# Differential attention's scores as three float32r products of split q and k

## The chip, the cores and the metric

One core of a Trainium2 chip runs the whole program. The metric is device time in microseconds (us) of one execution, lower is better; the profile is one execution, recorded instruction by instruction. TensorE (PE) multiplies matrices, VectorE (DVE) and ScalarE (ACT) work on rows, GpSimd (POOL) does very little here, and SyncE (SP) issues most of the DMAs that bring the weights from memory.

## What is computed

Two layers of a decoder trunk on 256 tokens of width 2048. In each layer one projection `w_in` feeds three kinds of head (differential attention, a gated linear recurrence "lru", chunked linear attention "gla"), one projection `w_out` joins them, and a SwiGLU feed-forward part follows. What the change touches is the scores of the differential attention, two maps `m` for each of 8 heads:

```python
q_d = rope(q_d.reshape(B, S, DIFF_HEADS, 2, DIFF_HD), pos)      # DIFF_HD = 64
k_d = rope(k_d.reshape(B, S, DIFF_HEADS, 2, DIFF_HD), pos)
...
s = jnp.einsum('bhmqd,bhmkd->bhmqk', q_blk * d ** -0.5, kh)     # q blocks of 128 rows
s = jnp.where(kpos[None, :] <= qpos[:, None], s, -jnp.inf)
p = jax.nn.softmax(s, axis=-1)
a = p[:, :, 0] - lam * p[:, :, 1]
o = rms_norm(jnp.einsum('bhqk,bhkv->bhqv', a, vh), subln_w) * (1.0 - lam_init)
```

## The kernel before

**Products.** Every large product is written as three float32r products: a float32 operand x is split into hi = float32r(x), made by ACT, and lo = x - hi, made by DVE, and hi·hi + hi·lo + lo·hi is summed in PSUM. `block` (lines 417 to 419) does this for one 512-wide (twice 264-wide) block of weights, 16 chunks of 128 rows, for the two token tiles t = 0, 1 in turn: six products a chunk. The tiles `hilo` hold the split weights, `split` makes them some 7 chunks ahead, and each costs ACT one cast and DVE one subtraction. A layer's input side is 12 such blocks ("in"); four blocks "op" of the output projection follow, chunks 0 to 7 of which read the attention's rows of `yh`, `yl`, chunks 8 to 11 the lru's and chunks 12 to 15 the gla's.

**Mixers.** Attention, lru and gla are generators (`head`, `norm`, `lru_x`, `lru_g`, `gla_gates`, `gla_out`, ...) whose steps are put between the products of the blocks. `rotated` transposes the rotated rows of q and of k (`tpq`), and ACT copies them to `s` tiles in float32. `head` (four heads in each of two groups g, two query tiles qt) multiplies q and k in float32 into `sps` (line 873), two maps on rows 0 to 63 and 64 to 127 of the array, adds the mask, takes exponentials (`e`), transposes them (`tpa`) and multiplies with v (`po`). At the layer's end `lru_g` transposes gate rows (`tp_lg`), multiplies (`lru`) and splits into `yh`, `yl` chunks 8 to 11; `gla_out` makes `pog` (two tiles), the squares of it on ACT (`junk`), the inverse root on DVE (`rs_v`, `rs_q`, `rr`), scaled rows (`ong`), the transpose (`tpog`) and the split into chunks 12 to 15.

**What sets the order.** A planner (`Lane`) runs while the program is written down. It keeps a clock `lane.clk`, which every PE step advances by an estimate of its cost, and an estimate of when DVE and ACT are free; after each unit of a block it lets the generators whose time has come issue their next step. The hardware's queues then run each engine's instructions in exactly that written order. So an estimate in the planner moves instructions, though nothing on the chip reads it. `lane.require` writes down a step at once when a block needs its result.

The score step and its estimate are:

```python
for m in range(2):
    r0 = slice(64 * m, 64 * m + 64)
    nc.tensor.matmul(sps[:, m, :nk], qT[r0, h, qt * P:(qt + 1) * P],
                     kT[r0, h, :nk], start=True, stop=True)
lane.clk += 0.45 if qt == 0 else 0.88
```

Of the kernel before, what the change touches and what calls it, by code (L numbers as in the profile page):

```python
# [10 lines left out]
F32 = mybir.dt.float32  # L11
F32R = mybir.dt.float32r
# [7 lines left out]
P = 128  # L20
S = 256
# [171 lines left out]
def tile_hybrid_trunk(ctx, tc, x, xT, w_in, w_out, w_gu, w_down, post_norms, lams,  # L193
                      vecs, wbd, w_gup, ropes, out):
    nc = tc.nc
    PS = bass.MemoryType.PSUM
    lane = Lane()
    done = lane.done
    dve, act = Engine(lane, nc.vector, 0.1, 1.04e-3), Engine(lane, nc.scalar, 0.1, 0.83e-3)
# [66 lines left out]
    for l in range(DEPTH):  # L266
# [5 lines left out]
        for kind, f, b in ffn_order():  # L272
# [4 lines left out]
            recipes, i = [], 0  # L277
# [300 lines left out]
    def parts(name):  # L578
        return pm.tile([P, DC, S], F32R, tag="big", name=name, bufs=5)

    def s4(name):
        return pm.tile([P, 4, S], F32, tag="s4", name="s4", bufs=NS4)

    def wide(name, tag="rp"):
        return pm.tile([P, 512], F32, tag=tag, name=name, bufs={"rp": 3, "e": 2, "on": 1}[tag])
# [154 lines left out]
    for l in range(DEPTH):  # L740
        lam_init = 0.8 - 0.6 * math.exp(-0.3 * l)
        sc, s2 = new_scale()
        yh, yl = None, None


        nlam = pt.tile([P, 1], F32, tag="nlam", name="nlam", bufs=2)
# [81 lines left out]
        def small(name, *needs):  # L828
            if name not in tiles:
                lane.require(*needs)  # L830
                tiles[name] = s4(name)
            return tiles[name]

        def rows(name, *needs):

            return small(name, *needs).rearrange("p a b -> p (a b)").rearrange("p (t n) -> p t n", t=NT)

        def rotated(made, scale, name):

            for t in range(NT):  # L840
                yield dve.through(0.25, "tr") if t == 0 else act.through(0.0, "tr")
                tp = turned(made[t], "tr", name="tpq")
                act.mul(small(name)[:, :, t * P:(t + 1) * P], tp, scale)
                act.drops("tr")
            done[name] = True

        def scaled(func, dst=None):
# [7 lines left out]
        def attention(g, qt):  # L855


            nk = (qt + 1) * P
            rsum = pt.tile([P, 4, 2], F32, tag="rsum", name="rsum")
            ssq = pt.tile([P, 4], F32, tag="ssq", name="ssq")  # L860
            po = []

            def head(h):
                prev = (l, g, qt, h - 1) if h else (l, g, 0, 3) if qt else (l, g - 1, 1, 3)
                yield 0.3, None, lane.has((l, "q", g), (l, "k", g), (l, "v", g), (l, "small"), (prev, "s"))
                yield 0.0, "sc", lambda: lane.use["e"] < 2
                done[(l, g, qt, h), "s"] = True
                lane.use["e"] += 1
                qT, kT, v = tiles[l, "q", g], tiles[l, "k", g], rows((l, "v", g))
                sps = pp.tile([P, 2, 512], F32, tag="sc", name="sps", bufs=1)  # L870
                for m in range(2):
                    r0 = slice(64 * m, 64 * m + 64)
                    nc.tensor.matmul(sps[:, m, :nk], qT[r0, h, qt * P:(qt + 1) * P],
                                     kT[r0, h, :nk], start=True, stop=True)
                lane.clk += 0.45 if qt == 0 else 0.88
                yield after(0.3)
                dve.tensor_tensor(out=sps[:, :, qt * P:nk], in0=sps[:, :, qt * P:nk],
                                  in1=cmask[:, None, :].to_broadcast([P, 2, P]), op=ALU.add)
                nm = pt.tile([P, 2], F32, tag="nm", name="nm")
                dve.tensor_reduce(out=nm, in_=sps[:, :, :nk], axis=AX.X, op=ALU.max, negate=True)  # L880
                yield dve.through()
                e = wide("e", "e").rearrange("p (m k) -> p m k", m=2)
                esum = pt.tile([P, 2], F32, tag="esum", name="esum")
                for m in range(2):
                    act.activation(e[:, m, :nk], sps[:, m, :nk], AF.Exp, bias=nm[:, m:m + 1],
                                         accum_out=esum[:, m:m + 1])
                act.drops("sc")
                yield act.through()
                dve.reciprocal(rsum[:, h, :], esum)
                yield NOW  # L890
                ncf = pt.tile([P, 1], F32, tag="ncf", name="ncf")
                dve.scalar_tensor_tensor(out=ncf, in0=esum[:, 0:1], scalar=nlam,
                                               in1=rsum[:, h, 1:2], op0=ALU.mult, op1=ALU.mult)
                yield NOW
                dve.scalar_tensor_tensor(out=e[:, 0, :nk], in0=e[:, 1, :nk], scalar=ncf,
                                               in1=e[:, 0, :nk], op0=ALU.mult, op1=ALU.add)
                yield dve.through(W_SM, "tr", lambda: lane.use["aT"] < 2)
                lane.use["aT"] += 1
                tp = pp.tile([P, 2, P], F32, tag="tr", name="tpa", bufs=1)
                for kt in range(qt + 1):  # L900
                    nc.tensor.transpose(tp[:, kt, :], e[:, 0, kt * P:(kt + 1) * P], ident)
                lane.use["e"] -= 1
                lane.clk += 0.11 * (qt + 1)
                aT = pt.tile([P, 2, P], F32, tag="aT", name="aT", bufs=2)
                act.copy(aT[:, :qt + 1, :], tp[:, :qt + 1, :])
                act.drops("tr")
                yield act.through(W_AT, ("o" if h == 0 else None), lane.has((prev, "av")))
                if h == 0:
                    po.append(pp.tile([P, 4, P], F32, tag="o", name="po", bufs=1))
                for kt in range(qt + 1):  # L910
                    nc.tensor.matmul(po[0][:, h, :], aT[:, kt, :], v[:, kt, h * P:(h + 1) * P],
                                     start=(kt == 0), stop=(kt == qt))
                lane.use["aT"] -= 1
                done[(l, g, qt, h), "av"] = True
                lane.clk += 0.22 * (qt + 1)
                yield after(0.3)
                junk = pt.tile([P, 512], F32, tag="junk", name="junk", bufs=1)[:, :P]
                act.activation(junk, po[0][:, h, :], AF.Square, accum_out=ssq[:, h:h + 1])
                yield act.through()
                done[(l, g, qt, h), "end"] = True  # L920

            def norm():
                yield 0.0, None, lane.has(*(((l, g, qt, h), "end") for h in range(4)))
                r0sq = pt.tile([P, 4], F32, tag="r0sq", name="r0sq", bufs=2)
                dve.tensor_tensor(out=r0sq, in0=rsum[:, :, 0], in1=rsum[:, :, 0], op=ALU.mult)
                rr = pt.tile([P, 4], F32, tag="rr", name="rr", bufs=2)
                yield NOW
                yield from rsqrt(rr, ssq, 4, 1.0 / P, pre=r0sq)
                dve.tensor_tensor(out=rr, in0=rr, in1=rsum[:, :, 0], op=ALU.mult)
                yield NOW  # L930
                on = wide("on", "on")
                dve.tensor_tensor(out=on.rearrange("p (h d) -> p h d", h=4), in0=po[0],
                                        in1=rr[:, :, None].to_broadcast([P, 4, P]), op=ALU.mult)
                dve.drops("o")
                yield dve.through(0.25, "tr")
                tp = turned(on, "tr", name="tpo")
                sl = slice(qt * P, (qt + 1) * P)
                split_scaled(yh[:, 4 * g:4 * g + 4, sl], yl[:, 4 * g:4 * g + 4, sl], tp, subw)
                dve.drops("tr")
                done[l, "y", g, qt] = True  # L940

            done[(l, -1, 1, 3), "s"] = done[(l, -1, 1, 3), "av"] = True
            for h in range(4):
                lane.add(10 + 2 * g + qt + h / 8, head(h))
            lane.add(9, norm())
# [63 lines left out]

        def lru_g(made, tiles):  # L1010
            for t in range(NT):
                yield act.through(0.25, "tr", lane.has((l, "hs")))
                hs = tiles["hs"]
                tp = turned(made[t], "tr", name="tp_lg")
                sl = slice(t * P, (t + 1) * P)
                dve.tensor_tensor(out=hs[:, :, sl], in0=hs[:, :, sl], in1=tp, op=ALU.mult)
                dve.drops("tr")
                yield dve.through()
                split_scaled(yh[:, 8:12, sl], yl[:, 8:12, sl], hs[:, :, sl], None)
                done[l, "lru", t] = True  # L1020
# [175 lines left out]
        for g in range(2):  # L1196
# [22 lines left out]
                    lane.add(6, small_parameters())  # L1219
                in_block(each(0, rotate, rotated, 1.0, (l, "k", g)), B_K[g][0])  # L1220
            in_block(each(0, scaled(AF.Copy, lambda t: rows((l, "v", g))[:, t, :]), ready, (l, "v", g)), B_V[g][0])
            if g == 0:
                yh, yl = parts("yh"), parts("yl")
            for qt in range(NT):
                attention(g, qt)
        in_block(each(4, scaled(AF.Copy), lru_x, tiles), B_LX[0])
# [274 lines left out]
```

## Time and profile before

| | us |
|---|---|
| median of three runs | 2192.33 (2191.77 to 2193.1) |
| the profiled execution's own time | 2193.04 |
| its span, first to last instruction | 2191.3 |
| PE busy | 2162.1 |
| DVE busy | 1814.0 |
| ACT busy | 1372.6 |

PE is the engine of the chain that ended last: the page puts 88% of that chain on PE and 8% on DVE. The granted clock is 0.999 of full speed throughout. "Busy" of PE counts products whose ends are modelled and which overlap, so the starts of successive products tell more than their lengths: a row that starts later than the usual step after the one above it marks a place where PE did not stream.

### The profile page before, as it was taken

How to read it: one execution, taken by the hardware profiler on the slowest of the kernel's cores; microseconds unless marked ns; L12 is line 12 of the kernel's file. 1: busy time of each engine (PE TensorE's matmuls, PEld its weight loads, DVE VectorE, ACT ScalarE, POOL GpSimd, SP SyncE). 2: the span in 40 equal slices, each digit the busy share in tenths (PEclk: the TensorE clock that was granted, in tenths of full speed). 3: DMA queues.
4: the chain of work that ended last, by engine and by line, in shares of the span. 5: the costliest groups of instructions: out<-in, count | busy, mean ns of one | idle time of the engine just before them, and what ended most of it. 6: DMA issues, size and time to landing. Idle time of an engine off the chain costs nothing.

```text
span 2191.3 us, 30890 instructions
## 1 busy us (share of the span) xinstructions
PE 2162.1 (99%) x10052; PEld 1769.5 (81%) x10052; DVE 1814.0 (83%) x3373; ACT 1372.6 (63%) x2715; POOL 96.1 (4%) x128
## 2 busy tenths in 40 slices
PE   8999999999999999999999999999999999999998
PEld 6778878887888888888877788788878888888886
DVE  6776965898999999999786668668989999999985
ACT  6556755676666666666565567557666666666663
POOL 0000000000000000000000000000000000000000
PEclk9999999999999999999999999999999999999999
DMA  8653646677877777777645536565777877777774
GB/s 285 193 165 111 212 153 217 201 217 233 253 241 245 240 243 237 240 236 245 217 147 158 179 108 217 170 208 180 240 231 241 258 240 244 242 238 238 240 233 140
DMA packets 202722, 467.32 MB, mean 213 GB/s; under 512 B 16416, under 2 KB 27200, under 8 KB 202560
## 3 DMA queue, kind: packets, MB, share of 16 engines
q1 hardware_dynamic: 186880, 434.93, 60.1%
q0 software_dynamic: 15104, 29.37, 7.9%
q8 instruction: 79, 1.29, 0.2%
q10 hardware_dynamic: 576, 1.05, 0.1%
q14 instruction: 83, 0.68, 0.1%
HBM read 463.18 MB, written 2.10 MB: 212 GB/s over the span
## 4 chain that ended last, share of the span: by engine, by line
PE 88%; DVE 8%; ACT 1%; issue 1%; DMA 1%; SPq 0%; DVEq 0%; ACTq 0%
PE in L417 6%; PE down L417 6%; PE down L419 6%; PE down L418 6%; PE in L419 6%; PE in L418 6%; PE gu_q L454 5%; PE gu_q L452 5%; PE gu_q L453 5%; PE gu_p L452 5%; PE gu_p L454 5%; PE gu_p L453 5%; DVE hilo L173 4%; PE op L419 2%; PE op L417 2%; PE op L418 2%
## 5 line engine op out<-in xcount | busy, mean ns | idle before, releaser
L173 DVE TENSOR_TENSOR hilo<-raw,hilo 128x512 fp32r<-128x512 f32 (+1 forms) x1472 | 957.3, 678 | 274.0 <-ACT hilo L173 267.9
L173 ACT CAST hilo<-raw 128x512 fp32r<-128x512 f32 (+1 forms) x1472 | 853.6, 614 | 274.7 <-PE gu_x L454 64.9
L173 ACT CAST hilo<-t 128x512 fp32r<-128x512 f32 x384 | 231.2, 621 | 152.1 <-DVE t L173 104.9
L417 PE MATMUL in<-hilo,hh 128*128 128x512 f32 (+1 forms) x768 | 301.1, 392 | 6.2 <-ACT hilo L173 6.1
L419 PE MATMUL in<-hilo,hl 128*128 128x512 f32 (+1 forms) x768 | 287.0, 374 | 0.8 <-DVE hl L173 0.8
L418 PE MATMUL in<-hilo,hh 128*128 128x512 f32 (+1 forms) x768 | 286.8, 373 | 0.6 <-DVE hilo L173 0.6
L417 PE MATMUL down<-hilo,hid 128*128 128x512 f32 x704 | 276.8, 393 | 4.5 <-DVE c_c L173 3.6
L419 PE MATMUL down<-hilo,hid 128*128 128x512 f32 x704 | 274.5, 390 | 1.0 <-DVE hid L173 1.0
L418 PE MATMUL down<-hilo,hid 128*128 128x512 f32 x704 | 274.0, 389 | 0.0
L173 DVE TENSOR_TENSOR hilo<-t,hilo 128x512 fp32r<-128x512 f32 x384 | 249.1, 690 | 2.9 <-ACT hilo L173 2.5
L417 PEld LDWEIGHTS in<-hilo,hh 128*128 128x128 f32 x768 | 144.6, 188 | 37.9 <-issue 6.7
L452 PE MATMUL gu_q<-hilo,hh 128*128 128x512 f32 x432 | 168.1, 389 | 0.0
L454 PE MATMUL gu_q<-hilo,hl 128*128 128x512 f32 x432 | 168.1, 389 | 0.0
L453 PE MATMUL gu_q<-hilo,hh 128*128 128x512 f32 x432 | 168.0, 389 | 0.0
L419 PEld LDWEIGHTS in<-hilo,hl 128*128 128x128 f32 x768 | 144.5, 188 | 27.5 <-DVE hl L173 1.3
L418 PEld LDWEIGHTS in<-hilo,hh 128*128 128x128 f32 x768 | 144.9, 189 | 22.9 <-DVE hilo L173 2.3
L417 PEld LDWEIGHTS down<-hilo,hid 128*128 128x128 f32 x704 | 132.2, 188 | 35.8 <-DVE c_c L173 4.9
L419 PEld LDWEIGHTS down<-hilo,hid 128*128 128x128 f32 x704 | 132.2, 188 | 29.7 <-DVE hid L173 1.8
L418 PEld LDWEIGHTS down<-hilo,hid 128*128 128x128 f32 x704 | 132.3, 188 | 26.4
L321 POOL DMA_DIRECT2D t<-in_w_gu_dram x96 | 83.0, 869 | 1189.2 <-DMA t<-in_w_gu_dram 1171.2
L173 DVE TENSOR_TENSOR t<-t,raw 128x512 f32<-128x512 f32 x192 | 132.3, 689 | 0.0
L452 PE MATMUL gu_p<-hilo,hh 128*128 128x512 f32 x320 | 124.9, 390 | 3.3 <-DVE hid L173 3.3
(239 smaller groups left out, 3333.1 us busy)
## 6 DMA issues: line engine op xcount, KB each, us to landing
raw<-in_w_gu_dram SPq DMA_DIRECT2D x352, 512.0 KB, 4.7
raw<-in_w_down_dram SPq DMA_DIRECT2D x176, 512.0 KB, 5.3
raw<-in_w_in_dram SPq DMA_DIRECT2D x159, 512.0 KB, 4.3
raw<-in_w_out_dram SPq DMA_DIRECT2D x64, 512.0 KB, 4.8
t<-in_w_gu_dram SPq DMA_DIRECT2D x96, 256.0 KB, 3.5
t<-in_w_gu_dram POOLq DMA_DIRECT2D x96, 256.0 KB, 6.7
raw<-in_w_in_dram SPq DMA_DIRECT2D x32, 264.0 KB, 2.8
gain<-in_post_norms_dram POOLq DMA_DIRECT2D x16, 256.0 KB, 4.3
```

Of the source, the lines that this page charges most:

```text
L173: return getattr(self.engine, name)(*args, **kwargs)
L321: nc.gpsimd.dma_start(out=o, in_=pieces[i + 1][:, 1, :], accum_op=ALU.add)
L417: nc.tensor.matmul(acc[t], ah, hi, start=(i == 0), stop=False)
L418: nc.tensor.matmul(acc[t], ah, lo, start=False, stop=False)
L419: nc.tensor.matmul(acc[t], al, hi, start=False, stop=(i == last))
L452: nc.tensor.matmul(acc, a[0], hi, start=start, stop=False)
L453: nc.tensor.matmul(acc, a[0], lo, start=False, stop=False)
L454: nc.tensor.matmul(acc, a[1], hi, start=False, stop=stop)
```

## The change

q and k are split like the large products' operands: `rotated` now calls `split_scaled`, so that ACT writes hi in float32r into the `s` tile and DVE writes lo = x·scale - hi into chunks 8 to 15 of `yh` (group 0) or `yl` (group 1), which nothing else uses until the lru and the gla are done. `yh` and `yl` are for this allocated at the layer's start. The PSUM tile of the transpose is handed on after DVE's step and not after ACT's. A head's two float32 products become six float32r products, hi·hi, hi·lo, lo·hi, the two maps in turn. `lru_g` also waits for the attention's last rows. The planner's estimate of the score step goes from 0.45 and 0.88 (qt 0 and 1) to 0.35 and 0.4.

```diff
-    def s4(name):
-        return pm.tile([P, 4, S], F32, tag="s4", name="s4", bufs=NS4)
+    def s4(name, dt=F32):
+        return pm.tile([P, 4, S], dt, tag="s4", name="s4", bufs=NS4)
...
-        yh, yl = None, None
+        yh, yl = parts("yh"), parts("yl")
...
-                tiles[name] = s4(name)
+                tiles[name] = s4(name, F32R if name[1] in ("q", "k") else F32)
             return tiles[name]
+
+        def low(name):
+
+            at = 8 if name[1] == "q" else 12
+            return (yh, yl)[name[2]][:, at:at + 4, :]
...
-                act.mul(small(name)[:, :, t * P:(t + 1) * P], tp, scale)
-                act.drops("tr")
+                ts = slice(t * P, (t + 1) * P)
+                split_scaled(small(name)[:, :, ts], low(name)[:, :, ts], tp, scale)
+                dve.drops("tr")
...
-                qT, kT, v = tiles[l, "q", g], tiles[l, "k", g], rows((l, "v", g))
+                q, k = ((tiles[l, n, g], low((l, n, g))) for n in "qk")
+                v = rows((l, "v", g))
                 sps = pp.tile([P, 2, 512], F32, tag="sc", name="sps", bufs=1)
-                for m in range(2):
-                    r0 = slice(64 * m, 64 * m + 64)
-                    nc.tensor.matmul(sps[:, m, :nk], qT[r0, h, qt * P:(qt + 1) * P],
-                                     kT[r0, h, :nk], start=True, stop=True)
-                lane.clk += 0.45 if qt == 0 else 0.88
+                for i, j in ((0, 0), (0, 1), (1, 0)):
+                    for m in range(2):
+                        r0 = slice(64 * m, 64 * m + 64)
+                        nc.tensor.matmul(sps[:, m, :nk], q[i][r0, h, qt * P:(qt + 1) * P],
+                                         k[j][r0, h, :nk], start=(i + j == 0), stop=(i == 1))
+                lane.clk += 0.35 if qt == 0 else 0.4
...
-                yield act.through(0.25, "tr", lane.has((l, "hs")))
+                yield act.through(0.25, "tr", lane.has((l, "hs"), (l, "y", 1, 1)))
...
-            if g == 0:
-                yh, yl = parts("yh"), parts("yl")
```

Because the planner's clock now runs slower against the count of products, steps that it places by time move to a later place in PE's queue. The order of the instructions shows it at three places. The names are those of the tiles written and read; `x4` counts equal rows.

DVE around the attention's last head of a layer (its `sps`, `nm`, `rsum`, `ncf`), among the lru's reciprocals, before:

```order
L173 TENSOR_SCALAR lru<-lru 128x256
L173 RECIPROCAL lru<-lru 128x128
L173 TENSOR_TENSOR sps<-sps,cmask 128x2x128
L173 TENSOR_REDUCE nm<-sps 128x2
L173 TENSOR_TENSOR hilo<-raw,hilo 128x264 x4
L173 RECIPROCAL lru<-lru 128x128
L173 TENSOR_TENSOR hilo<-raw,hilo 128x264 x2
L173 TENSOR_SCALAR lru<-lru 128x256
L173 RECIPROCAL lru<-lru 128x128
L173 TENSOR_TENSOR hilo<-raw,hilo 128x264 x2
L173 RECIPROCAL rsum<-esum 128x2
L173 SCALAR_TENSOR_TENSOR ncf<-esum,nlam,rsum 128x1
```

The same head on DVE now:

```order
L173 TENSOR_TENSOR sps<-sps,cmask 128x2x128
L173 TENSOR_REDUCE nm<-sps 128x2
L173 TENSOR_TENSOR hilo<-raw,hilo 128x264 x2
L173 TENSOR_SCALAR lru<-lru 128x256
L173 RECIPROCAL lru<-lru 128x128
L173 TENSOR_TENSOR hilo<-raw,hilo 128x264 x4
L173 RECIPROCAL lru<-lru 128x128
L173 TENSOR_TENSOR hilo<-raw,hilo 128x264 x2
L173 RECIPROCAL rsum<-esum 128x2
L173 SCALAR_TENSOR_TENSOR ncf<-esum,nlam,rsum 128x1
```

One reciprocal that stood ahead of the head stands behind it; ahead of the group's `on` there were seven reciprocals of the layer's eight and are now six.

ACT where the last "in" block ends (`sb` are that block's gate rows, `s_2357` the gla's gate, `pog` the gla's first tile), before:

```order
L173 CAST hilo<-raw 128x512 x4
L173 ACT_TABLE_LOAD
L173 ACTIVATE s_2357<-s_2357 128x1024
L173 CAST hilo<-raw 128x512 x2
L173 ACTIVATE junk,ssq<-pog 128x128 x4
L173 CAST hilo<-raw 128x512
L173 ACT_TABLE_LOAD
L173 ACTIVATE sb<-in_2786,scale 128x512
L173 ACTIVATE sb<-in_2787,scale 128x512
L173 CAST hilo<-raw 128x512 x5
```

The same stretch of ACT now:

```order
L173 CAST hilo<-raw 128x512 x5
L173 ACT_TABLE_LOAD
L173 ACTIVATE sb<-in_2857,scale 128x512
L173 ACT_TABLE_LOAD
L173 ACTIVATE s_2428<-s_2428 128x1024
L173 ACT_TABLE_LOAD
L173 ACTIVATE sb<-in_2858,scale 128x512
L173 CAST hilo<-raw 128x512
L173 ACTIVATE junk,ssq<-pog 128x128 x4
L173 CAST hilo<-raw 128x512 x5
```

The gla's gate, which stood ahead of both gate rows, stands between them, with a table load more on either side, and the squares of the first gla tile stand behind. Over the program ACT has 30 table loads, 24 before. On PE the gla's first tile moved from 12 products ahead of the block's end to 3 products behind it.

ACT at the end of the gla, up to its last split, before:

```order
L173 CAST yh<-lru 128x4x128
L173 CAST hilo<-raw 128x512
L173 ACTIVATE junk,ssq<-pog 128x128 x4
L173 CAST hilo<-raw 128x512 x5
L173 ACTIVATE yh<-tpog,vec 128x4x128
```

And now:

```order
L173 CAST yh<-lru 128x4x128
L173 ACTIVATE yh<-tpog,vec 128x4x128
L173 CAST hilo<-raw 128x512 x2
L173 ACTIVATE junk,ssq<-pog 128x128 x4
L173 CAST hilo<-raw 128x512 x2
L173 ACTIVATE yh<-tpog,vec 128x4x128
```

Five weight casts stood between the squares of the second gla tile and its split, two do now. On PE 30 products stood between that tile and its transpose `tpog`, 12 do now; `tpog` itself stands where it stood, in front of chunk 12 of the first "op" block. The first `tpog` stands between the two token tiles of chunk 8, behind both `tp_lg`; before, it stood between them.

## Rows read from the trace of the kernel before

**Rows 1.** Windows: us, PE, PEld, DVE, ACT, POOL busy (count), clock, DMA

```profile
77.00:103.00 26.00, 26.00 (x126) 19.43 (x124) 18.24 (x49) 15.70 (x51) 0.00 (x0) 1.00 0.49 139
```

**Rows 2.** Timeline, first score group: start, length, engine, line, operation, tiles, shape, count

```profile
77.35 0.39 PE L419 MATMUL in<-hilo,hl 128*128 128x512 f32 x1
...
77.67 0.49 PE L873 MATMUL sps<-s,s 64*128 64x128 f32 x4
...
78.09 0.50 PE L417 MATMUL in<-hilo,hh 128*128 128x512 f32 x1
...
78.42 0.39 PE L418 MATMUL in<-hilo,hh 128*128 128x512 f32 x1
...
77.78 0.19 PEld L873 LDWEIGHTS sps<-s,s 64*128 64x128 f32 x2
```

**Rows 3.** Timeline of PE, a score group with 256 columns

```profile
103.02 0.70 PE L873 MATMUL sps<-s,s 64*128 64x256 f32 x4
...
103.65 0.50 PE L417 MATMUL in<-hilo,hh 128*128 128x512 f32 x1
```

**Rows 4.** Timeline of PE in the 264-wide blocks; in brackets idle time, what ended it

```profile
226.12 0.28 PE L418 MATMUL in<-hilo,hh 128*128 128x264 f32 x1
226.24 0.28 PE L419 MATMUL in<-hilo,hl 128*128 128x264 f32 x1
227.13 0.41 PE L901 MATMUL tpa<-ident,e 128*128 128x128 f32 x2 [0.61 <-DVE e L173]
227.29 0.37 PE L417 MATMUL in<-hilo,hh 128*128 128x264 f32 x1
...
238.50 0.63 PE L574 MATMUL tpo<-ident,on 128*128 128x128 f32 x4 [0.43 <-DVE on L173]
```

**Rows 5.** Groups by form: operation, tiles, shapes, count | busy us, mean ns | idle before

```profile
L173 DVE SCALAR_TENSOR_TENSOR yl<-tpo,subw,yh 128x512 fp32r<-128x512 f32 x8 | 6.0, 746 | 0.0
...
L173 ACT ACT_TABLE_LOAD x23 | 29.5, 1283 | 5.7 <-DVE scale L173 5.3
...
L173 ACT ACTIVATE s<-s 128x1024 f32<-128x1024 f32 x2 | 2.1, 1057 | 0.0
```

**Rows 6.** Timeline, the end of layer 0's lru and gla

```profile
294.26 1.27 ACT L173 ACTIVATE sb<-in,scale 128x512 f32<-128x512 f32 x2
...
299.77 1.90 DVE L173 TENSOR_TENSOR hilo<-raw,hilo 128x512 fp32r<-128x512 f32 x3
...
304.13 0.60 PE L574 MATMUL tp_lg<-ident,sb 128*128 128x128 f32 x4
...
304.76 0.69 DVE L173 TENSOR_TENSOR lru<-lru,tp_lg 128x512 f32<-128x512 f32 x1 [0.64 <-PE tp_lg L574]
...
307.60 0.50 PE L417 MATMUL op<-hilo,yh 128*128 128x512 f32 x1
...
307.77 0.28 ACT L173 ACTIVATE junk<-pog 128x128 f32<-128x128 f32 x1 [1.15 <-PE pog L1160]
...
309.24 2.69 ACT L173 CAST hilo<-raw 128x512 fp32r<-128x512 f32 x5
...
310.49 0.16 DVE L173 TENSOR_SCALAR rs_v<-ssq 128x4 f32<-128x4 f32 x1
...
313.84 1.12 DVE L173 SCALAR_TENSOR_TENSOR ong<-pog,rr,s 128x128 f32<-128x128 f32 x4
...
314.54 0.81 PE L574 MATMUL tpog<-ident,ong 128*128 128x128 f32 x4
...
315.38 0.69 ACT L173 ACTIVATE yh<-tpog,vec 128x512 fp32r<-128x512 f32 x1 [3.45 <-PE tpog L574]
...
316.11 0.75 DVE L173 SCALAR_TENSOR_TENSOR yl<-tpog,vec,yh 128x512 fp32r<-128x512 f32 x1
...
316.91 0.50 PE L419 MATMUL op<-hilo,yl 128*128 128x512 f32 x1
```

## The prediction

> **What bounds the kernel now.** I read the page first (PE busy almost all the span, and 88% of the last chain on PE), then windows through the attention's stretch, then the starts of PE's rows around the places that the change touches. In a window of the attention PE is busy 26.0 of 26.0 us and DVE 18.2 [rows 1]. So the kernel is as long as PE's queue: own work, plus the few places where PE, in its fixed order, waits for DVE or ACT. A change pays or costs only by what it does to PE's own work, or by a step that comes to stand in PE's queue too early for the engine that feeds it. The second is the larger here.
>
> The units: from 307.60 to 314.54 PE runs 30 products of 512 columns, the first with 0.11 for its load [rows 6]: (6.94 - 0.11)/30 = 0.228 us each. Products of 264 columns step by 0.12 [rows 4].
>
> **The change part by part.**
>
> *The score products.* There are 32 heads' groups in all, 16 with 128 columns and 16 with 256. A float32 product is recorded as two passes; the two maps run side by side. The first group [rows 2]: its first load starts at 77.67, the second pass's loads at 77.78, and the next block's load at 78.09. So a load takes 0.11, and two passes with the emptying of the array take 0.31, of which the passes, at 0.105 each by the next row, are 0.21. With 256 columns 103.02 to 103.65 is 0.63 [rows 3] against 0.42: two passes of 0.21, so the passes go by columns. A float32r product of 128 columns is not in the trace. The slope between 264 and 512 columns, (0.228 - 0.12)/248 = 0.43 ns a column, gives 0.06 for 128 and 0.117 for 256. Three pairs, each load (0.108) running under the pair before it: 128 columns take 3 × 0.108 + 0.06 = 0.385 from the first load, against 0.108 + 2 × 0.105 = 0.32 before, **+0.063**; 256 columns take 0.108 + 3 × 0.117 = 0.46 against 0.108 + 2 × 0.213 = 0.535, **-0.076**. Over 16 of each: **-0.2 us**. Fewer passes by columns, more loads, and the two cancel. Bounds: if no load binds, 0.108 + 3 × 0.06 and the same 0.46, 16 × (-0.03 - 0.076) = -1.7; if the maps do not run side by side, six loads in a row make 0.71 and six passes make 0.81, 16 × (0.39 + 0.275) = +10.6; if 128 columns go at float32's rate for one full product, 3 × 0.213 + 0.108 = 0.75, which is +6.8 - 1.2 = +5.6. I take the slope's value, since the 264-column row is the nearest.
>
> A load under a running product of the same rows is what the rows show: the second pass's loads start at 77.78, while the first pass runs [rows 2]. The Trainium skill says otherwise (TensorE: Matmul & The Clock Gate, Part 3, "What overlaps and what doesn't"): a load overlaps a product in flight only where the row groups differ. By that each row group pays load plus product three times, 0.507 and 0.675; that is a rival below.
>
> *The splits.* 16 subtractions more on DVE, two for each of q and k, group and layer. The nearest row is the attention's own split from PSUM, 0.746 us [rows 5]: 11.9 us of DVE. ACT's step only changes its type. They fall in the first five blocks of a layer, where DVE has 7.8 us free of 26 [rows 1]; even six in one such window are 4.5 us. And the first score stands after the V block's end in both orders; I cost them at **0**. Without that cover they would cost at most 11.9.
>
> *The moved steps ahead of the layer's end.* PE waits 0.61 for the last head's `e` and 0.43 for `on`, both DVE's [rows 4], twice in the program: 2.1 us. Now one reciprocal and its companion fewer stand ahead of either. Some of this goes; between 0 and -2.1 I take **-1.6**.
>
> *The layer's end: the gla's second tile.* Before, from the end of `pog` (307.60) to the product that reads the split's lo (316.91) pass 9.31 us [rows 6]. PE's own work in it is 35 products and `tpog`, 35 × 0.228 + 0.44 = 8.4; it waits 0.9. The chain beside it: squares begin at 307.77 and are done at 309.24, DVE's root begins at 310.49 behind weight subtractions, `ong` 313.84, `tpog`, `yh` 315.38, `yl` 316.11 to 316.86. In the new order the same chain has squares 1.64, one cast and subtraction 1.2 (0.54 and 0.63), twelve root steps at 0.2, one subtraction 0.6, `ong` 1.1, the rest of `tpog` 0.35, ACT 0.8, DVE 0.8: 8.9. But 12 products stand beside it instead of 30, so PE has 17 × 0.228 + 0.44 = 4.3 of its own. It waits 4.6 instead of 0.9: **+3.7 a layer**. Bounds: 1.8 less if the two weight steps get out of the way; as long as before, +0.4.
>
> *The layer's end: the lru at chunk 8.* Count from the first "op" product. ACT: first gate rows done at 0.15, table 1.28, gate 1.06, table 1.28 [rows 5], second gate rows 0.63 [rows 6], end 4.4; a cast, squares, two casts: 7.75. DVE subtracts until 8.5, then the first `lru` product (ready earlier: PE's `tp_lg` ends at 7.65, after 18 products, `pog`, which takes 307.60 - 304.13 - 0.44 = 3.0 [rows 6], and itself) until 9.1. Then DVE's row in the new order: weight step 0.6, eight root steps 1.6, weight step 0.6, four root steps 0.8, `ong` 1.04, weight step 0.6, `yl` 0.66, weight step 0.6, second `lru` product 0.65, two weight steps 1.2, `yl` 0.66: 18.1. PE reaches the product that reads it at 7.65 + 35 × 0.228 + 2 × 0.47 = 16.5. **+1.6 a layer**, where before PE came to it without a wait. Bounds: 0 to 3.
>
> Products moved from behind the gla's tile to ahead of it cost nothing; PE does them in any case. The FFN's instructions stand in the same order, so nothing is given back there.
>
> *Sum:* 2 × (3.7 + 1.6) - 1.6 - 0.2 = **+8.8 us**. The profiled execution took 2193.04 (span 2191.3 and 1.7 around it), so 2201.8; the median lies 0.7 lower: **2201**.
>
> **The rivals.**
>
> *Late by little (chance 0.16).* DVE gets through its root without weight steps in the way: the second wait grows by 1.9, the one at chunk 8 is covered. For it: in the window of the attention DVE was free for 7.8 us of 26 [rows 1], so its queue may run ahead of what I lay out. Against: the new order writes them between the root steps. 2201 - 2 × 3.4 = 2194, no change.
>
> *The narrow products are dear (0.12).* By the bounds above +5.8 or +10.8 against my value: 2207 to 2212. For it: no row has float32r at 128 columns or on half the rows. Against: nothing in the 264-column step hints at it.
>
> *Loads wait within a row group (0.06)*, the page's rule: 16 × (0.12 + 0.215) = +5.4, 2206. Against it the load at 77.78.
>
> *Not slower: the gap around the group goes (0.06).* A group costs more than its passes. It begins 0.32 after the last product's start and not 0.23, its first load and the block's next load (78.09, with L418 0.33 later) are not hidden, and the array empties before 78.09: 0.09 + 0.11 + 0.10 + 0.11 = 0.41 us [rows 2], 13.1 over 32 groups. If that is the price of changing between float32 and float32r, it vanishes, and 2201 - 13 = 2188. It decides from 8.8/32 = 0.275 a group. Against: the float32 transposes over the whole array, `tpa` at 227.13, are followed by the next product after 0.16 [rows 4], so the gap belongs to the half-height products, which stay. The Trainium skill agrees (TensorEngine Tiling (Array Packing), Tiling Modes): a change of tiling mode drains TensorE.
>
> **How the numbers follow.** The forecast, 2201 with 2197 to 2205 of its own, has 0.60. About 0.2% (4.4 us) is what a measurement of this kernel can tell from no change. Slower by more, above 2196.7: the forecast 0.60, the two dear cases 0.18, the upper edge of the first rival 0.03, so 0.81. Within: 0.13 of the first rival and 0.01 of the last, 0.14. Faster: 0.05, the last. The range leaves out the last rival (0.06), the upper half of the dear products (0.06) and the first rival's lower edge (some 0.06): 2194 to 2210.
>
> **What would show it.** In the changed kernel's timeline a score group of 128 columns from first load to next block's load some 0.48 (0.42 before), of 256 some 0.55 (0.63 before). PE's waits: `e` and `on` shorter than 0.61 and 0.43; in the first "op" block of each layer `tpog` standing 3 to 4 us behind the product ahead of it, and about 1.5 us lost at chunk 8. DVE's busy time up by 12 us, ACT's by six table loads, 7.7 us. I am wrong if the score groups take over 0.7 us, if the "op" block has no new wait, or if new waits appear among the lru's steps, where DVE and ACT are full and steps have moved too.

## The result: 11.4 us slower, and the profile after

The changed kernel takes **2203.9 us** (median; 2202.79 to 2204.98), the kernel before beside it 2192.53 (2191.77 to 2193.10): a ratio of **1.0052**, 95% interval 1.004 to 1.0063. The forecast was 2201, slower, between 2194 and 2210. The profiled execution took 2204.98, 11.94 more than that of before.

The first part of the page after:

```profile
span 2202.9 us, 31010 instructions
...
PE 2168.8 (98%) x10116; PEld 1776.1 (81%) x10116; DVE 1822.3 (83%) x3389; ACT 1378.4 (63%) x2721; POOL 95.9 (4%) x128
```

The span is 11.6 longer, but PE is busy only 6.7 longer (2162.1 before), DVE 8.3 and ACT 5.8: some 5 us of the loss are a PE that stands, and the rows below show that part of the busy time is slow.

**Where it went.** The 9120 wide products stand in the same order in both kernels, so the start of the n-th of them says how far each kernel has come.

| stretch, by the starts of its first and last product | before, us | after, us | difference |
|---|---|---|---|
| layer 0, attention: from the fourth "in" block, where the scores begin, to the 11th | 163.89 | 163.32 | -0.57 |
| layer 0, end: 11th and 12th "in" and first "op" block | 80.57 | 87.20 | **+6.63** |
| layer 1, the attention as above | 163.87 | 163.32 | -0.55 |
| layer 1, end as above | 80.61 | 87.33 | **+6.72** |

The two ends give 13.35, the attention takes back 1.12: 12.23. The fourth block of layer 0 started 0.31 earlier (76.58 against 76.90), which leaves the 11.9 of the profiled executions. That start is no effect of the change: in the profiles of the twelve kernels of this document it lies between 76.1 and 77.9, also where nothing ahead of it differs. So what is worth less than 1 us is better read from such stretches than from whole times.

**The score groups.** PE's rows and one of its weight loads (PEld) at the first group, 128 columns, and PE's rows at one with 256, in the timeline of after (they answer to [rows 2, 3]; the columns are start, length, engine, line, operation, tiles, shape, count):

```profile
77.03 0.39 PE L419 MATMUL in<-hilo,hl 128*128 128x512 f32 x1
77.35 0.33 PE L881 MATMUL sps<-s,s 64*128 64x128 f32 x2
77.46 0.19 PEld L881 LDWEIGHTS sps<-yh,s 64*128 64x128 f32 x2
77.52 0.28 PE L881 MATMUL sps<-yh,s 64*128 64x128 f32 x2
77.63 0.28 PE L881 MATMUL sps<-s,yh 64*128 64x128 f32 x2
77.83 0.50 PE L417 MATMUL in<-hilo,hh 128*128 128x512 f32 x1
78.17 0.39 PE L418 MATMUL in<-hilo,hh 128*128 128x512 f32 x1
```

```profile
103.56 0.38 PE L881 MATMUL sps<-s,s 64*128 64x256 f32 x2
103.78 0.28 PE L881 MATMUL sps<-yh,s 64*128 64x256 f32 x2
103.90 0.28 PE L881 MATMUL sps<-s,yh 64*128 64x256 f32 x2
104.11 0.50 PE L417 MATMUL in<-hilo,hh 128*128 128x512 f32 x1
```

From first load to next block's load: 77.35 to 77.83 is 0.48, 103.56 to 104.11 is 0.55, as forecast (0.42 and 0.63 before). The pairs of products follow one another at 0.11 with 128 columns and at 0.12 with 256. The second load starts at 77.46, while the first pair is still at work (the second pair starts only at 77.52), so loads run under products of the same rows: a load of 0.108 and a product of 0.117 (the prediction's values), one after the other, would put pairs of 256 columns 0.225 apart.

**The layer's end.** PE's rows around chunk 8 and around the gla's second `tpog`, after (they answer to [rows 6]):

```profile
305.11 0.39 PE L419 MATMUL op<-hilo,yl 128*128 128x512 f32 x1
305.59 0.66 PE L574 MATMUL tpog<-ident,ong 128*128 128x128 f32 x4
...
306.58 0.40 PE L418 MATMUL op<-hilo,yh 128*128 128x512 f32 x1
307.39 0.50 PE L419 MATMUL op<-hilo,yl 128*128 128x512 f32 x1 [0.42 <-DVE yl L173]
...
314.78 0.39 PE L419 MATMUL op<-hilo,yl 128*128 128x512 f32 x1
318.43 1.25 PE L574 MATMUL tpog<-ident,ong 128*128 128x128 f32 x4 [3.26 <-DVE ong L173]
319.33 0.77 PE L417 MATMUL op<-hilo,yh 128*128 128x512 f32 x1
319.90 0.63 PE L418 MATMUL op<-hilo,yh 128*128 128x512 f32 x1
...
323.74 0.53 PE L418 MATMUL op<-hilo,yh 128*128 128x512 f32 x1
324.11 0.39 PE L419 MATMUL op<-hilo,yl 128*128 128x512 f32 x1
```

Both new waits stand where the forecast put them. At chunk 8 the rows from 305.11 to 307.39 take 2.28, where three products at 0.228 and a `tpog` at 0.44 would take 1.12: **1.15** lost. At the second `tpog` PE stands from the end of its last product (314.78 + 0.228) to 318.43, **3.42**. What nobody forecast comes behind it: eleven products, 319.33 to 323.74, start 0.43 apart instead of 0.228. Windows over that stretch (us, busy PE, PEld, DVE, ACT, POOL with counts, granted clock, DMA share, GB/s):

```profile
315.01:318.43 3.42, 0.16 (x2) 0.01 (x1) 2.96 (x16) 0.00 (x0) 0.00 (x0) 0.82 0.44 153
318.43:319.33 0.90, 0.90 (x5) 0.67 (x5) 0.71 (x3) 0.00 (x0) 0.00 (x0) 0.50 0.00 0
319.33:324.11 4.78, 4.78 (x13) 3.69 (x13) 2.55 (x4) 2.23 (x4) 0.00 (x0) 0.51 0.22 65
324.11:329.00 4.89, 4.89 (x23) 4.02 (x22) 1.57 (x3) 2.29 (x6) 0.00 (x0) 1.00 0.46 155
```

The granted clock is 0.50 to 0.51 until 324.11, the 1.2 GHz level, and then 1.00, 2.4 GHz. PE's busy column reads full in the slow stretch: those eleven products take 4.78 instead of 2.51, so **2.27** of the loss counts as busy time. Layer 1 repeats it (`tpog` stands 3.62 behind the product ahead of it, 3.65 here, and eleven slow products and a part of a twelfth follow).

### The profile page after: what moved, and what is told of

The parts are those of the page before. It is cut to its first block, busy times and chain, and to the rows that moved or that the text cites. A ratio compares the mean times of both kernels' runs of the same rounds, so it can differ in the third digit from the quotient of the medians.

```text
span 2202.9 us, 31010 instructions
## 1 busy us (share of the span) xinstructions
PE 2168.8 (98%) x10116; PEld 1776.1 (81%) x10116; DVE 1822.3 (83%) x3389; ACT 1378.4 (63%) x2721; POOL 95.9 (4%) x128
## 4 chain that ended last, share of the span: by engine, by line
PE 87%; DVE 8%; ACT 2%; issue 1%; DMA 1%; SPq 0%; DVEq 0%; ACTq 0%
PE in L417 6%; PE down L417 6%; PE down L419 6%; PE down L418 6%; PE in L419 6%; PE in L418 6%; PE gu_q L453 5%; PE gu_q L452 5%; PE gu_q L454 5%; PE gu_p L452 5%; PE gu_p L454 5%; PE gu_p L453 5%; DVE hilo L173 4%; PE op L419 2%; PE op L417 2%; PE op L418 2%
## 5 line engine op out<-in xcount | busy, mean ns | idle before, releaser
L173 DVE TENSOR_TENSOR hilo<-raw,hilo 128x512 fp32r<-128x512 f32 (+1 forms) x1472 | 954.5, 675 | 271.7 <-ACT hilo L173 266.3
```

Source lines behind the costliest of these rows:

```text
L173: return getattr(self.engine, name)(*args, **kwargs)
```

## The experiments

"With old estimates" means 0.45 and 0.88 for a score step on the planner's clock, as before the change; the change makes them 0.35 and 0.40. Every ratio is against runs of the kernel before on the same chip.

### The change in two halves

The new score products under the old estimates:

```diff
-                lane.clk += 0.35 if qt == 0 else 0.4
+                lane.clk += 0.45 if qt == 0 else 0.88
```

> The changed kernel with the planner's estimate of a score step put back to 0.45 and 0.88; scores, splits and everything else as changed. Theory A, it is the places in PE's queue: the end of the layer stands again as in the kernel before (five weight casts between the last squares and the split, 30 products ahead of the second gla transpose), the 3.4 us wait there goes, and the time is 2192.5 - 0.2 for the score products = 2192 (2191 to 2194). Theory B, it is the added work (16 subtractions on DVE, the transpose's PSUM tile held until DVE is done, six loads a head): the loss stays, 2203 to 2204.

Measured 2191.36, ratio 0.9993 (0.9984 to 1.0003). By the stretches of the table the ends are as before, and the attention is 0.6 quicker in each layer: a wait of 0.56 of a `po` for ACT (at 119.89 before) is gone. And the new estimates alone, in the kernel before, with its float32 scores:

```diff
-                lane.clk += 0.45 if qt == 0 else 0.88
+                lane.clk += 0.35 if qt == 0 else 0.4
```

> The kernel before, with float32 scores and no split of q and k, and only the planner's estimate changed to 0.35 and 0.4. Theory A: the end of the layer stands as in the changed kernel and the loss comes with the number alone, 2192.5 + 11.4 + 0.2 = 2204 (2202 to 2206). Theory B: no added work, so 2192 to 2193.

Measured 2202.22, ratio 1.0042 (1.0027 to 1.0057). The loss is the two numbers, which nothing on the chip reads. PE's rows at the gla's second `tpog`, first with the new products and old estimates, then with the new estimates alone:

```profile
313.44 0.39 PE L419 MATMUL op<-hilo,yl 128*128 128x512 f32 x1
313.67 0.81 PE L574 MATMUL tpog<-ident,ong 128*128 128x128 f32 x4
```

```profile
313.71 0.39 PE L419 MATMUL op<-hilo,yl 128*128 128x512 f32 x1
317.32 1.10 PE L574 MATMUL tpog<-ident,ong 128*128 128x128 f32 x4 [3.21 <-DVE ong L173]
...
318.49 0.39 PE L418 MATMUL op<-hilo,yh 128*128 128x512 f32 x1
318.72 0.54 PE L419 MATMUL op<-hilo,yl 128*128 128x512 f32 x1
...
320.64 0.63 PE L417 MATMUL op<-hilo,yh 128*128 128x512 f32 x1
321.07 0.63 PE L418 MATMUL op<-hilo,yh 128*128 128x512 f32 x1
```

With the old numbers `tpog` follows the product ahead of it by 0.23; with the new ones it waits, under either arithmetic, and products 0.43 apart follow. Here there are fewer of them: the granted clock is still 1.00 from 317.32 to 318.82, over `tpog` and the next products (318.49 and 318.72, 0.23 apart), and 0.50 from there to 322.23, for seven products; in layer 1 there are five. So the ends cost 6.1 and 5.3 by the stretches, not 6.6 and 6.7, and the attention takes back 1.3 in each layer (0.6 in the changed kernel, where that `po` still waits).

How the numbers compare with the real cost: a group lengthens PE's row by the time from the product ahead of it to the second product behind it, less two steps: 78.17 - 77.03 - 2 × 0.228 = 0.68, and for 256 columns 104.45 - 103.24 - 2 × 0.228 = 0.75 by the same rows. Eight groups of each in a layer take 11.5 us. The old estimates sum to 10.6, the new ones to 6.0, so in the changed kernel the planner's clock falls 5.5 us a layer behind PE. Falling behind is not what costs, though. In the run further down that issues every set of score products twice, with the old estimates, the groups take 1.02 and 1.11, so the planner's clock falls 6.3 us a layer behind; but it writes the same order as with one set, and `tpog` follows the product ahead of it by 0.23. The numbers act by the order that comes of them. Estimates near the real cost:

```diff
-                lane.clk += 0.35 if qt == 0 else 0.4
+                lane.clk += 0.60 if qt == 0 else 0.68
```

> The changed kernel with the planner's estimate of a score step at 0.60 and 0.68 us, near what the trace of the changed kernel shows for a score group with its neighbours, instead of 0.35 and 0.4. The layer's end is then written in the order of the kernel before (the gla's second pog well ahead of its tpog). If the lost time is only the places at the layer's end: 2191 to 2192, no wait of tpog over 0.6 us. If the exact values matter throughout the layer (the middle steps of the lru and the reciprocals), it should differ from the run with the old estimates, 2191.4, by over 2 us either way. If the three products themselves cost what was lost, about 2200.

Measured 2192.66, ratio 1.0000 (0.9991 to 1.0009): within 1.3 us of the run with the old estimates, and no wait at `tpog`. It is the places that decide.

### The half clock behind the wait

Twelve extra products of 512 columns, whose result nobody reads, ahead of the second `tpog` of each layer:

```diff
+                if t == 1:
+                    fill = pp.tile([P, 512], F32, tag="o", name="fill", bufs=1)
+                    for _ in range(12):
+                        nc.tensor.matmul(fill, yh[:, 0, 0:P], yh[:, 0:2, :], start=True, stop=True)
```

> The changed kernel with 12 extra products of 512 columns (2.7 us, their result unused) on PE just ahead of the second gla transpose of each layer, inside the 3.4 us in which PE waits there. Theory C, the clock: after the wait ten to eleven products run at 0.427 us instead of 0.228, which is 2.1 us a layer of the 5.7; with PE at work the rows after it keep to 0.228 and the time falls by about 4, to 2200 (2198.5 to 2201.5). If the slow products have another cause, the time stays at 2204 or rises, by up to 5 us if the extra products do not fit into the wait.

Measured 2202.03, ratio 1.0042 (1.0028 to 1.0056), about 2 us less than the changed kernel although it does 5.5 us more work (24 × 0.228). PE's rows of the timeline:

```profile
315.39 2.88 PE L1191 MATMUL fill<-yh 128*128 128x512 f32 x12
318.79 1.10 PE L574 MATMUL tpog<-ident,ong 128*128 128x128 f32 x4 [0.52 <-DVE ong L173]
319.65 0.48 PE L417 MATMUL op<-hilo,yh 128*128 128x512 f32 x1
...
320.20 0.40 PE L419 MATMUL op<-hilo,yl 128*128 128x512 f32 x1
320.67 0.50 PE L417 MATMUL op<-hilo,yh 128*128 128x512 f32 x1
321.00 0.40 PE L418 MATMUL op<-hilo,yh 128*128 128x512 f32 x1
321.46 0.50 PE L419 MATMUL op<-hilo,yl 128*128 128x512 f32 x1
```

And the window from 318 to 324 (columns as above):

```profile
318.00:324.00 6.00, 5.35 (x22) 3.40 (x21) 3.92 (x10) 2.23 (x4) 0.00 (x0) 1.00 0.19 58
```

The wait is filled, the clock stays at 1.00 and products keep their 0.23. So the standing PE is what the clock fell for. The gain is smaller than expected, and the rows say why: at full speed PE comes to the readers of `yh` and `yl` early and waits for them (starts 320.20 to 320.67 and 321.00 to 321.46, 0.24 and 0.23 more than a step). At half speed these waits were hidden in the slow products. Also `tpog` keeps its 0.86 (0.90 in the changed kernel) at full clock: it paces itself by the four `ong`, and is not slow on account of the clock.

### Chunk 8 and the table loads

The gla gate's Silu, which stands between the two gate rows on ACT and costs a table load on either side, issued ahead of the transposes of k:

```diff
+                if c == 0:
+                    act.activation(sgo, sgo, AF.Silu)
...
-            act.activation(sgo, sgo, AF.Silu)
```

> The changed kernel with the gla gate's Silu issued ahead of the transposes of k, so that ACT does not load a table between the first and the second gate rows of the lru (two table loads fewer a layer). If the wait at chunk 8 comes from those two loads and the gate between the rows: it goes, 1.06 us a layer; but PE then comes to the second tpog sooner, with 6 products in place of 10 between it and its pog, and by the working of the prediction the wait there grows by what PE no longer does beside it, 1.4 us a layer: together 2204 to 2205. If the table loads also hold up the gla's own chain, the second wait does not grow: 2201 to 2202.

Measured 2203.35, ratio 1.0048 (1.0035 to 1.0062), a little under the expected 2204 to 2205. PE's rows at chunk 8, and at the second `tpog`:

```profile
306.01 0.39 PE L419 MATMUL op<-hilo,yl 128*128 128x512 f32 x1
306.24 0.60 PE L574 MATMUL tpog<-ident,ong 128*128 128x128 f32 x4
...
307.14 0.40 PE L419 MATMUL op<-hilo,yl 128*128 128x512 f32 x1
...
314.42 0.40 PE L419 MATMUL op<-hilo,yl 128*128 128x512 f32 x1
319.19 1.25 PE L574 MATMUL tpog<-ident,ong 128*128 128x128 f32 x4 [4.37 <-DVE ong L173]
```

The lost time at chunk 8 is gone (306.01 to 307.14 is 1.13), so the loads and the gate between the rows were its cause. `tpog` stands 4.77 behind the product ahead of it instead of 3.65, 1.1 more (0.9 in layer 1): with less work beside it, 6 products instead of 12 (the expectation says 10), the same chain shows more of itself. That is the rule by which the forecast priced this wait, and by it the six products were worth 1.4.

### Undoing only the layer's end

The changed kernel, small estimates kept, with time added to the planner's clock just before the last "in" block, first 3 us, then 1.5:

```diff
+        lane.clk += 3
```

> The changed kernel, its small estimates kept, with one line more: 3 us are added to the planner's clock just before the layer's last input block. All up to that block stands as in the changed kernel; from there on the gla's second pog and its tpog have 36 products between them, against 10 in the changed kernel. If the layer's end alone costs the time: the wait of 3.4 us, the products at half clock behind it (2.1) and the wait at chunk 8 (1.06) go, 2 x 6.6 = 13.1 us less, and small waits of the yh and yl steps come back as they stand in the kernel before (about 0.9 a layer): 2203.9 - 13.1 + 1.8 = 2192.6 at most, and down to 2190, since in the attention the changed order is 0.6 us a layer quicker than before. If the small estimates cost time in the middle of the layer too: 2195 or more.

Measured 2192.89, ratio 0.9999 (0.9991 to 1.0008): the 11 us are gone with a line that touches only the layer's end. It is at the top of what was expected (0.3 above), and new waits show why it is no lower, those of the gla's gate sums, in both layers; layer 0:

```profile
267.83 0.71 PE L1113 MATMUL psa<-s 64*128 64x128 f32 x8 [0.26 <-DVE s L173]
...
271.79 0.39 PE L419 MATMUL in<-hilo,hl 128*128 128x512 f32 x1
273.22 0.72 PE L1113 MATMUL psa<-s 64*128 64x128 f32 x8 [1.05 <-DVE s L173]
```

> The changed kernel with 1.5 us, in place of 3, added to the planner's clock ahead of the layer's last input block. The gla's second pog then stands 30 products ahead of its tpog, as in the kernel before, and the gate's sums psa stand later than with 3 us. If the 2.1 us that psa waited in the first layer of the run with 3 us are what that run lost again: psa waits less than 0.5 us, and the whole takes 2190 to 2191, a little under the run with the old estimates (2191.4). If instead the long waits go but the earlier steps of the gla cost the same elsewhere: 2192.5 to 2193.

Measured 2192.21, ratio 0.9996 (0.9987 to 1.0005). The expectation of 2190 to 2191 fell: of the two `psa` the first no longer waits, but the second still starts 1.26 behind the product ahead of it (0.79 in layer 1; 0.32 in both layers of the kernel before), and the small waits at `yh` and `yl` are back. No version here is faster than the kernel before by more than a measurement shows; the lowest is the one with the old estimates.

### The price of the score products by itself

Each head's set of score products issued twice, writing the same numbers again: the three float32r products under the old estimates, and the float32 products of the kernel before.

```diff
-                for i, j in ((0, 0), (0, 1), (1, 0)):
+                for i, j in ((0, 0), (0, 1), (1, 0)) * 2:
```

> The changed kernel with the old estimates (0.45 and 0.88) and the six score products of a head issued twice; the second set starts and stops its own sum and writes the same numbers again. It measures the price of the score products by themselves, against the run with the old estimates, 2191.4. A set takes three pitches: 3 x 0.108 for 128 columns and 3 x 0.117 for 256, so 16 x (0.324 + 0.351) = 10.8 us if all of it lies on the path: 2202.2. If the waits that follow a score group (for the exponentials) take some of it up, less: 2197 to 2201. If a set costs more than its pitches (a gap between sums): 2204 or more.

```diff
-                for m in range(2):
+                for m in (0, 1, 0, 1):
```

> The kernel before, with float32 scores, with the two score products of a head issued twice (the second pair starts its own sum and writes the same numbers again). Beside the run of the three products twice (+10.0 us over the same kernel with one set), it gives the price of what the change takes away. A set of float32 products is two passes, 0.105 each for 128 columns and 0.213 for 256, if the second set's loads run under the passes ahead of them: 16 x (0.21 + 0.43) = 10.2 us, 2203; then three narrow products and two float32 passes cost the same, and the change cannot win on TensorE. If the loads are not hidden (0.108 more a set, or 0.22 where neither pass hides one): 13.6 to 17.3, 2206 to 2210. If the waits that follow a group take some of it up: 2200 to 2202.

Measured 2201.36 against 2191.36 with one set, **10.0 us** for a set of three float32r products (10.3 if each is first taken against the kernel before beside it, 8.63 above and 1.66 below); and 2202.94 against 2192.35, **10.6 us** for a set of float32 ones. PE's rows at the first group of either:

```profile
78.66 0.33 PE L881 MATMUL sps<-s,s 64*128 64x128 f32 x2
...
79.05 0.28 PE L881 MATMUL sps<-s,s 64*128 64x128 f32 x2
...
79.48 0.50 PE L417 MATMUL in<-hilo,hh 128*128 128x512 f32 x1
```

```profile
77.86 0.72 PE L873 MATMUL sps<-s,s 64*128 64x128 f32 x8
78.50 0.50 PE L417 MATMUL in<-hilo,hh 128*128 128x512 f32 x1
```

The second set costs 0.82 - 0.48 = 0.34, three steps of 0.11, and 0.64 - 0.42 = 0.22, two passes of 0.11, at 128 columns. With 256 columns it is 0.35 and 0.43. Over 16 groups of each that makes 11.0 and 10.5 us by PE's rows. By the stretches of the table, which leave out the start, the second sets cost 10.0 and 9.7: the wait for the last head's `e` gives about the rest back (0.69 falls to 0.25 in each layer, and 0.62 to 0.08 with float32). So score work lies on the path all but in full. Which kind of set is the dearer is not shown, since the stretches put it 0.3 us one way and the medians 0.6 the other; the first sets, by their rows (0.48 + 0.55 against 0.42 + 0.63), differ by 0.3 over the program. There was next to nothing to win on TensorE.

### Map after map

The change writes the two maps' products in turns. Here the three of map 0 come first, then the three of map 1:

```diff
-                for i, j in ((0, 0), (0, 1), (1, 0)):
-                    for m in range(2):
+                for m in range(2):
+                    for i, j in ((0, 0), (0, 1), (1, 0)):
```

> The changed kernel with the order of a head's six products turned: three of map 0, then three of map 1, instead of in turns; the planner's estimates and so all other places are the same. If the two maps run side by side only because they come in turns (one pair in flight, the third product of map 0 beside the first of map 1 at best), a group of 128 columns takes 0.2 to 0.27 more and one of 256 columns 0.23 to 0.35 more, 32 groups 7 to 10 us: 2211 to 2214. If each half of the array takes its own products whatever the order, 2204.

Measured 2204.28, ratio 1.0052 (1.0037 to 1.0067): the same as the changed kernel. PE's rows:

```profile
77.57 0.33 PE L881 MATMUL sps<-s,s 64*128 64x128 f32 x2
77.73 0.28 PE L881 MATMUL sps<-yh,s 64*128 64x128 f32 x2
77.85 0.28 PE L881 MATMUL sps<-s,yh 64*128 64x128 f32 x2
78.06 0.50 PE L417 MATMUL in<-hilo,hh 128*128 128x512 f32 x1
```

The profile shows them in pairs all the same (`s,s` twice, `yh,s` twice, `s,yh` twice), 0.49 for the group. The two halves of the rows each follow their own products; the order between the halves in the program did not matter. So "exactly that written order" holds on TensorE for the products of one half of the rows, not between the halves.

## Why the prediction was right, point by point

- **What bounds the kernel**: right. PE's queue in its fixed order; the two score sets issued twice show added PE work all but in full (10.0 us of 11.0). Moved places cost by waits, and by the half clock behind one of them, which is not in this picture.
- **Score products, -0.2**: right. 0.48 and 0.55 a group as worked out, -0.3 in all; the two runs that double a set tell no difference between the kinds. The rivals fall by the same rows: narrow products are not dear, a load does start under a running product of its own row group (77.46), and the gap around a group is as it was (0.32 ahead of it, 77.03 to 77.35, and 0.34 behind, 77.83 to 78.17), so nothing came back there. The Trainium skill (TensorE: Matmul & The Clock Gate, Part 3, "What overlaps and what doesn't"), which the prediction weighed, has it that a load overlaps a running product only where the row groups differ. This trace does not agree: 0.12 from pair to pair with 256 columns, not 0.225.
- **Splits, 0**: right. They are 16 rows of some 0.687, 11.0 us of DVE, and the run that has them under the old estimates is not slower. DVE's whole busy time rose by 8.3 only and ACT's by 5.8, not by 12 and 7.7, since other rows became a little shorter: the 1472 subtractions `hilo<-raw` took 954.5 instead of 957.3. Why they did is open.
- **Moved steps, -1.6**: right in kind, too large. The stretches give 1.12 in both layers together, and that holds the score products too. The wait for `e` [rows 4] is gone and that for `on` is 0.29 instead of 0.43; but a `tpa` of an earlier head (at 142.65) now stands 0.19 behind its step.
- **Chunk 8, +1.6 a layer**: right in place and cause, 1.15 in size. The wait that was forecast, at the product that reads `yl`, is 0.58 of it; the rest is the first `tpog`, which starts 0.25 late and takes 0.31 longer, and which the working did not name. Both go with the table loads.
- **The gla's second tile, +3.7 a layer**: the step that was mis-sized. The chain was priced at 8.9 and took 9.0 (`pog` ends at 312.15, `yl` at 321.18), and `tpog` stood 3.65 behind as foretold. But the working let the products behind the wait run at full speed. They ran at half the clock: 3.42 of standing, 0.46 more for a `tpog` that follows the four `ong`, and 2.27 in slow products, less the 0.9 of before, is 5.25. That is 1.55 a layer more than forecast, 3.1 in all, and makes up the miss: 8.8 + 3.1 - 0.9 for the two chunks 8 (0.45 each) + 0.7 for the attention is 11.7, against 11.9 of the profiled executions and 11.4 of the medians. That the 0.9 too much at chunk 8 hides a part of the clock's cost is luck. So is the length of the slow stretch: with seven and five slow products, in the run with the estimates alone, the two ends cost 11.4, 1.9 less.
- **The rival "late by little"** would have needed the wait at chunk 8 covered and that at `tpog` short; neither was. Nor did new waits appear among the lru's steps, the last of the signs that the forecast named.

## What to carry to other kernels

When an operation is replaced, price the planner's or scheduler's estimate as a change of its own: here the arithmetic cost nothing and a number that no engine reads cost 11 us, because a layer's last dependent chain lost the work that stood beside it. The step takes 0.68 and 0.75 from PE's queue, with its gaps; 0.35 and 0.40 are near its products alone. But being nearer to the truth is not what repaired the order: 0.60 and 0.68 did, and so did the old 0.45 and 0.88. What has to be looked at is the order that comes out, first of all what stands between the links of a layer's last chain. And a wait of a few us on TensorE costs more than itself: look at the starts of the products behind it, and at the granted clock there, since the busy column hides that loss.

## What was new about the hardware

- After PE stood for 3.4 us the granted clock was 0.50, and stayed so for eleven products (0.427 each instead of 0.228). The number does not follow the length of the wait: with the estimates alone PE stood as long in both layers (3.4 us), and seven and five slow products followed, in layer 0 only after PE had been at work again for 1.5 us; in the run with the gate's Silu moved, longer waits, of 4.5 in layer 0 and 4.3 in layer 1, were followed by six and by ten. With twelve products in the wait, and 0.68 of it left, there were none.
- Two maps on the two halves of the array's rows ran side by side even where the program writes all of one map ahead of the other.
- Pairs of float32r products on half the rows step by 0.11 with 128 columns, like their loads, and by 0.12 with 256: half the columns saved next to nothing.
